# A decoder trunk on eight cores: the start of layer 0 reordered, the evictions of the convolution stage regrouped, and the norm at the head of the feed-forward part moved

## The chip, the cores and the metric

The kernel runs on the eight cores of one Trainium2 chip, which are two dies of four cores (0 to 3 and 4 to 7). Each core computes its own share of the requests, with the same program. The time is the device time of the slowest core in microseconds (us). A run is called slow where one die was over 1% longer than the other at a lower TensorE clock, or where it was over 1.5% above the fastest run of the same kernel.

The engines are named as in the profile: PE is TensorE, PEld its weight load, DVE is VectorE, ACT is ScalarE, POOL is GpSimd, and SP issues transfers (the page gives it no busy time, and the timeline shows its issues as SPq).

## The reference, cut to what matters

```python
def trunk(x, pool_prev, conv_prev, ffn_prev, pos0, p):
    for l in range(DEPTH):                                   # 4 layers
        h = rmsnorm(x, p['norm1'][l])
        z = h @ p['w_in'][l]                                 # 1024 -> 1792 columns, groups A, B, C
        a_out, pst = pool_mix(za, ...)                       # windows 2, 4, 8, 16
        b_out = spatial_gate(zu, zv, ...)                    # chunks of 128
        c_in = zc[..., :D_C] * jax.nn.sigmoid(zc[..., D_C:])
        c_conv, cst = causal_dwconv(c_in, conv_prev[l], ...) # depthwise, width 31
        c_out = jax.nn.silu(layernorm(c_conv, ...))
        x = x + jnp.concatenate([a_out, b_out, c_out], axis=-1) @ p['w_out'][l]
        h2 = rmsnorm(x, p['norm2'][l])
        up = h2 @ p['w_up'][l]                               # 1024 -> 2 x 2816
        gate_c, fst = causal_dwconv(gate, ffn_prev[l], ...)  # width 3
        x = x + (jax.nn.silu(gate_c) * val) @ p['w_down'][l]
    return rmsnorm(x, p['final_norm']), ...
```

A core holds 2048 prompt tokens and 64 sample tokens (x is kept transposed, 8 blocks of 128 channels). They are handled in five tiles: tiles 0 to 3 have 512 prompt tokens each, and tile 4 has the 64 sample tokens.

## The kernel before

A small scheduler in the program issues the instructions in order for each engine and works out the semaphore waits. A PSUM bank is marked as exclusive, so that a read of it also waits for every earlier read by another engine:

```python
    def _deps(self, reads, writes):
        for r in reads:
            if r.w is not None ...:      # wait for the last write
            if r.excl:                   # PSUM banks: wait for the other engines' reads too
                for s, v in r.r.items(): ...
```

**The start.** SP issues its loads in the order in which they are written here (from 1.06 us on; the state data at 22.97 and 25.40, the constants at 26.66). The tiny state data that the state casts need, and the constants of the pooling chains, are loaded behind most of x and of the staged weights:

```python
        load_x(4)
        S.dma("sp", VT[:, 0:VT_FW], vt_d[:, 0:VT_FW], DM["vt"], ...)     # norm gains
        for i in range(4):                                               # four f32 weights, cast later
            stage(X[:, :, 1024 + 256 * i : ...], [Res(f"stg{i}")])
            if i == 0:
                load_x(0, 0, 4); load_x(0, 4, 8)
        load_x(1, 0, 4); load_x(1, 4, 8)
        # ... (cut)
        stp = state_dma(0)                                               # sz, sc
        S.dma("sp", CST[:], cst_d, DM["cst"], ...)                       # constants
        nrm.first(4)                                                     # squares and sum of tile 4
        cast(0, "act", 0, 4); cast(0, "dve", 4, 8)                       # first weight to bf16
        nrm.apply(4, range(KC)); nrm.first(0); nrm.apply(0, range(KC))
        for i in range(1, 4): cast(i, "pool")
        # ... x tiles 2 and 3 behind the casts (cut)
        S.dma("pool", OBM[:], oneb_d, DM["obm"], ...)
        for t in range(6): bands.load(t)                                 # convolution matrices, 480 KB each
        # at the top of every layer:
            for j in range(3):                                           # state casts
                S.op("act", lambda e: e.copy(cin[j][:, 0:4, MB:MW], sc_v[...]), reads=[Rsc], writes=[Rcin[j]])
```

The projections of layer 0 then go by tile in the order 0, 4, 1, 2, 3, each tile through all five units (two for pooling, three for the gated convolution input), and each tile's norm just ahead of it. After the third convolution block's input has been sent through DRAM and back (a "hop", which transposes it), `prep_dma(0)` loads the spatial-gate matrices and `prep(0)` masks them on DVE.

**The convolution stage.** There are 12 steps. In each, PE forms two halves of 272 columns in two PSUM banks, and the result is needed as f32 (`y`), as bf16 (`yb`) and squared. The LayerNorm sums of a step (`stats`) are matmuls that run one step later:

```python
                for h in range(2):
                    cb = CVQ[:, 2 * q + h:2 * q + h + 1]
                    yh, ph, Rph = y[:, h * MW:(h + 1) * MW], pb2[h][0][:, 0:MW], pb2[h][1]
                    yb = ybf[:, 2 * (q % 2), h * MW:(h + 1) * MW]
                    if h == 0:
                        S.op("act", lambda e: e.activation(yh, ph, AF.Identity, bias=cb), ...)          # L795
                    else:
                        S.op("dve", lambda e: e.tensor_scalar(yh, ph, cb, None, ALU.add), ...)          # L797
                    S.op("dve", lambda e: e.tensor_scalar(yb, ph, cb, None, ALU.add), ...)              # L798
                b = 2 * (q % 2)
                S.op("act", lambda e: e.activation(ybf[:, b + 1, :], y, AF.Square), ...)                # L800
                if q >= 1:
                    stats(q - 1)                                                                        # PE, L755
```

**The head of the feed-forward part.** The last tile's norm is not finished when the up-projections begin. `tail2[0]` is its sum on PE (L415) with Ln and Exp on ACT, `tail2[1]` and `tail2[2]` scale its two halves on DVE. `up` leaves each unit's Silu pending until the next unit:

```python
                    for i, (f, ti) in enumerate(seq):
                        up(f, f, ti, w01[f], tail2[0] if i == 1 else None)    # between the two matmul groups of unit 1
                        if i == 2:
                            tail2[1]()
                        if i == 3:
                            tail2[2]()
```

Of the kernel before, what the change touches and what calls it, by code (L numbers as in the profile page):

```python
# [7 lines left out]
BF16 = mybir.dt.bfloat16  # L8
# [5 lines left out]
KC = 8  # L14
# [212 lines left out]
def build_nc():  # L227
# [39 lines left out]
    with ExitStack() as st:  # L267
# [57 lines left out]
        DXH = [S.dsem(f"dxh{t}") for t in range(2)]  # L325
# [45 lines left out]
        S.op("dve", lambda e: e.memset(EPST[:], EPS), writes=[Rones])  # L371
        load_x(4)
        S.dma("sp", VT[:, 0:VT_FW], vt_d[:, 0:VT_FW], DM["vt"], writes=[Rvt])
        for i in range(4):
            c = 1024 + 256 * i
            stage(X[:, :, c:c + 256], [Res(f"stg{i}")])
            if i == 0:
                load_x(0, 0, 4)
                load_x(0, 4, 8)
# [3 lines left out]
        class Norm:  # L383
            def __init__(self, base, gcol, final=False):
# [4 lines left out]
                sq_v, self.Rsq = AR.carve("sq", base + 256, 3 * 512, 3)  # L389
                self.sq = sq_v.rearrange("p (a n) -> p a n", a=3)  # L390
                self.ac, self.Rac = AR.carve("ac", base + 1792, 512, 1)
# [6 lines left out]
            def sqr(self, ti, m):  # L398
                c0, n = TTS[ti]
                q = self.q % 3  # L400
                self.q += 1
                sq = self.sq[:, q, 0:n]
                S.op("act", lambda e: e.activation(sq, X[:, m, c0:c0 + n], AF.Square), reads=[RX[m][ti]], writes=[self.Rsq[q]])  # L403
                if m == 0:
                    self.prev[ti] = (sq, self.Rsq[q])
                    return
                in0, R0 = self.prev[ti]
                dst, Rd = (self.ab[ti == 4][:, 0:n], self.Rab[ti == 4]) if m == KC - 1 else (self.ac[:, 0:n], self.Rac[0])
                S.op("pool", lambda e: e.tensor_tensor(dst, in0, sq, ALU.add), reads=[R0, self.Rsq[q]], writes=[Rd])  # L409
                self.prev[ti] = (dst, Rd)  # L410
# [14 lines left out]
            def apply(self, ti, kcs):  # L425
                c0, n = TTS[ti]
                ri, Rpb, i = self.ri[ti]
                for kc in kcs:
# [4 lines left out]
                    if self.final and kc % 4 == 3:  # L433
                        out_dma(y_o[:, kc - 3:kc + 1, c0:c0 + n], X[:, kc - 3:kc + 1, c0:c0 + n], [RX[k][ti] for k in range(kc - 3, kc + 1)], "y")
# [3 lines left out]
            def direct(self, ti, m):  # L438
                c0, n = TTS[ti]
                q = self.q % 3  # L440
                self.q += 1
                sq = self.sq[:, q].bitcast(BF16)[:, 0:n]
                S.op("act", lambda e: e.activation(sq, X[:, m, c0:c0 + n], AF.Square), reads=[RX[m][ti]], writes=[self.Rsq[q]])
# [10 lines left out]

            def first(self, ti, kcs=range(KC)):
                c0, n = TTS[ti]
                sqb = self.sq.rearrange("p a n -> p (a n)").bitcast(BF16).rearrange("p (a n) -> p a n", a=6)
                if kcs[0] == 0:
                    self.ri[ti] = bank(True)
                pb, Rpb, i = self.ri[ti]  # L460
                for kc in kcs:
                    q = kc % 3
                    eng = "act" if kc % 2 == 0 else "dve"
                    dst = sqb[:, 2 * q, 0:n]
                    src = X[:, kc, c0:c0 + n]
                    if eng == "act":
                        S.op("act", lambda e: e.activation(dst, src, AF.Square), reads=[RX[kc][ti]], writes=[self.Rsq[q]])
                    else:
                        S.op("dve", lambda e: e.tensor_tensor(dst, src, src, ALU.mult), reads=[RX[kc][ti]], writes=[self.Rsq[q]])
                    S.op("pe", lambda e: e.matmul(pb[:, 0:n], ONES[:], dst, start=(kc == 0), stop=(kc == KC - 1)),  # L470
                         reads=[self.Rsq[q], Rones], writes=[Rpb])
                if kcs[-1] == KC - 1:
                    self.rsq(ti, pb, Rpb, i)
# [48 lines left out]
        S.dma("sp", CST[:], cst_d, DM["cst"], writes=[Rcst])  # L522
        nrm.first(4)
        cast(0, "act", 0, 4)
        cast(0, "dve", 4, 8)
        nrm.apply(4, range(KC))
        nrm.first(0)
        nrm.apply(0, range(KC))
        for i in range(1, 4):
            cast(i, "pool")  # L530
        for t in (2, 3):
            after("sp", stages[2 * t - 4][1] + stages[2 * t - 3][1])
            load_x(t)
        S.dma("sp", VT[:, VT_FW:VT_N], vt_d[:, VT_FW:VT_N], DM["vt2"], writes=[Rvt2])
        const_dma(0)
        S.dma("pool", OBM[:], oneb_d, DM["obm"], writes=[Robm])
        qst = stq_dma(0)
        W.fill(5)
        bands = Bands(0)
        for t in range(6):  # L540
            bands.load(t)

        for l in range(DEPTH):
            sz_v, Rsz, sc_v, Rsc = stp
            QS, Rqs = qst
            cin, Rcin = [], []
            for j, a in enumerate((0, 4 * MW, 5308)):
                v, r = AR.carve(f"cin{j}", a, 4 * MW, 1)
                cin.append(v.bitcast(BF16).rearrange("p (f m) -> p f m", f=8))
                Rcin += r  # L550
# [6 lines left out]
            for j in range(3):  # L557
                S.op("act", lambda e: e.copy(cin[j][:, 0:4, MB:MW], sc_v[:, 64 * j:64 * j + 64].rearrange("p (f m) -> p f m", f=4)),
                     reads=[Rsc], writes=[Rcin[j]])
# [103 lines left out]
            def hop_in(j):  # L663
# [4 lines left out]
                S.dma("sp", hop1[j].rearrange("g (c f) m -> (g c) (f m)", f=8), cin[j].rearrange("p f m -> p (f m)"), DH1[j], reads=[Rcin[j]], writes=[Rh1[j]])  # L668
                S.dma("sp", Q[j][:, :, 4:4 + MW], hop1[j].rearrange("g p m -> p g m"), DQ[j], reads=[Rh1[j]], writes=[Rq[j][0]])

            if l == 0:
# [634 lines left out]
```

## Time and profile before

| | before |
|---|---|
| median of the first three runs | 2824.86 us (2819.37 to 3251.31) |
| profiled run, slowest core (4) | 2821.3 us |
| spans of die 0 / die 1 (medians) | 2791.5 / 2816.4 us |
| mean granted PE clock of die 0 / die 1 | 0.988 / 0.977 |
| PE busy | 2704.7 us, 96% |
| layer 0: first projection / first convolution matmul / start of the next stage | 23.6 / 138.6 / 172.2 us |
| convolution stage, layers 1 to 3 | 27.1, 27.5, 27.1 us |

The page, the table of stretches, the waits of PE and the timeline at the start are shown in the prediction below, where they are read. The stage starts in this table and further down are read from the trace as the start of the first matmul of each stage.

One part of the old profile is needed that the prediction only tells in words, the timeline of core 4 in the convolution stage of layer 1. Columns: start and length in us, engine and line, operation, out<-in, and in brackets the idle time before it and what ended it. First DVE, then ACT:

```profile
830.15 0.50 DVE L798 TENSOR_SCALAR arena<-ps,cvq_s 128x272 bf16<-128x272 f32 x1 [0.90 <-PE ps L755]
830.57 0.49 DVE L797 TENSOR_SCALAR arena<-ps,cvq_s 128x272 f32<-128x272 f32 x1
831.17 0.50 DVE L798 TENSOR_SCALAR arena<-ps,cvq_s 128x272 bf16<-128x272 f32 x1
832.50 0.50 DVE L798 TENSOR_SCALAR arena<-ps,cvq_s 128x272 bf16<-128x272 f32 x1 [0.83 <-PE ps L755]
...
831.15 0.66 ACT L800 ACTIVATE arena<-arena 128x544 bf16<-128x544 f32 x1 [1.11 <-DVE arena L797]
831.90 0.49 ACT L795 ACTIVATE arena<-ps,cvq_s 128x272 f32<-128x272 f32 x1
```

From one L798 to the same place a step later is 2.35 us, of which DVE works some 1.5. The bracket at 832.50 names PE's sums, but the program makes L798 wait until ACT's L795 has left the first half's bank: L795 ends at 832.39, and L798 begins 0.1 us later. L795 itself stands in ACT's queue behind the square L800 of the step before (831.15 + 0.66, L795 begins at 831.90), and L800 can't begin until DVE has written the second half (it stood 1.11 us). The sums on PE wait for both engines.

### The profile page before, as it was taken

To read this page: it belongs to the slowest core of one execution; us is meant where nothing else is said; L and a number is where in the kernel's file an instruction comes from. 1 tells how busy PE (TensorE), PEld (TensorE's weight loads), DVE (VectorE), ACT (ScalarE), POOL (GpSimd) and SP (SyncE) were. 2 spreads that over 40 slices of the span, in tenths; PEclk is the share of its full clock that TensorE was granted. 3 is DMA by queue.
4 is the path that set the end of the run, shared out by engine and by line. 5 is a ranking of instruction groups with operands and counts; after the bars stand their busy time and mean duration, and the time that the engine had idled before them with its cause. 6 is when DMAs were issued, how large, how long until landed. Compare 5 with 4: busy or idle time off the path is not lost.

```text
span 2821.3 us, 49230 instructions; the slowest of 8 cores (2789.2 to 2821.3 us)
## 1 busy us (share of the span) xinstructions
PE 2704.7 (96%) x15467; PEld 1317.9 (47%) x15735; DVE 1776.7 (63%) x3023; ACT 1436.0 (51%) x2758; POOL 535.5 (19%) x845
## 2 busy tenths in 40 slices
PE   4889999999999999999999999999999999999997
PEld 1354444444455444444445544444444644444443
DVE  3666755656685765656577576564668666555566
ACT  2354735447425572727634466372753647364573
POOL 1025100000603500000331430000041350000003
PEclk8899999999999999999999999999999999999998
DMA  9152412122445222221515322222242513122113
GB/s 227 63 113 39 68 30 44 29 46 44 80 90 112 34 37 36 42 38 31 93 38 105 83 48 35 45 35 38 38 79 65 121 30 58 32 45 41 31 36 124
DMA packets 82702, 170.97 MB, mean 61 GB/s; under 512 B 10960, under 2 KB 41936, under 8 KB 82384
## 3 DMA queue, kind: packets, MB, share of 16 engines
q0 software_dynamic: 31568, 108.44, 23.1%
q1 hardware_dynamic: 50880, 59.35, 7.0%
q8 instruction: 133, 2.18, 0.3%
q14 instruction: 121, 0.99, 0.1%
HBM read 250.37 MB, written 28.39 MB: 99 GB/s over the span
## 4 chain that ended last, share of the span: by engine, by line
PE 89%; DVE 4%; issue 3%; ACT 1%; DMA 1%; SPq 1%; POOL 0%; DVEq 0%; ACTq 0%; POOLq 0%
PE ps L1055 23%; PE ps L1049 22%; PE ps L981 15%; PE ps L1125 14%; PE ps L822 3%; PE ps L919 3%; PE ps L639 3%; PE ps L633 3%; PE ps L566 2%; DVE H L430 1%; SPq L138 1%; PE ps L905 1%; DVE arena L797 1%; DMA cstt<-cst 1%; PE ps L755 1%
## 5 line engine op out<-in xcount | busy, mean ns | idle before, releaser
L1055 PE MATMUL ps<-H,wsall 128*128 128x512 bf16 (+1 forms) x3500 | 707.9, 345 | 1.1
L1049 PE MATMUL ps<-H,wsall 128*128 128x512 bf16 (+1 forms) x3404 | 696.5, 344 | 6.2
L1069 DVE SCALAR_TENSOR_TENSOR arena<-arena,vt_s 128x512 f32<-128x512 f32 (+1 forms) x440 | 289.6, 658 | 406.4 <-ACT arena L1068 389.3
L1064 ACT COPY arena<-ps 128x512 f32<-128x512 f32 (+1 forms) x440 | 224.0, 509 | 582.8 <-PE ps L1049 534.3
L981 PE MATMUL ps<-arena,wsall 128*128 128x512 bf16 (+1 forms) x2515 | 474.7, 348 | 2.6
L1049 PEld LDWEIGHTS ps<-H,wsall 128*128 128x128 bf16 x3520 | 304.3, 99 | 339.7 <-issue 26.3
L1055 PEld LDWEIGHTS ps<-H,wsall 128*128 128x128 bf16 x3520 | 304.5, 99 | 339.0 <-issue 25.6
L1125 PE MATMUL ps<-arena,wsall 128*128 128x512 bf16 (+1 forms) x2200 | 399.0, 341 | 2.1
L1068 ACT ACTIVATE arena<-ps,vt_s 128x512 f32<-128x512 f32 (+1 forms) x440 | 309.2, 703 | 66.4 <-ACT arena L1064 3.0
L981 PEld LDWEIGHTS ps<-arena,wsall 128*128 128x128 bf16 x2560 | 217.9, 99 | 250.5 <-issue 44.4
L409 POOL TENSOR_TENSOR arena<-arena 128x512 f32<-128x512 f32 (+2 forms) x273 | 293.6, 1075 | 176.8 <-ACT arena L403 146.5
L1071 DVE SCALAR_TENSOR_TENSOR arena<-arena,vt_s 128x512 f32<-128x512 f32 (+1 forms) x440 | 289.6, 658 | 45.9 <-DVE arena L1069 0.2
L1128 DVE TENSOR_TENSOR X<-ps,X 128x512 f32<-128x512 f32 (+1 forms) x320 | 184.7, 596 | 196.9 <-PE ps L1125 196.9
L403 ACT ACTIVATE arena<-X 128x512 f32<-128x512 f32 (+1 forms) x312 | 168.0, 551 | 261.3 <-DVE X L983 146.9
L1125 PEld LDWEIGHTS ps<-arena,wsall 128*128 128x128 bf16 x2240 | 188.4, 98 | 211.5
L983 DVE TENSOR_TENSOR X<-ps,X 128x512 f32<-128x512 f32 (+1 forms) x320 | 185.0, 594 | 142.2 <-PE ps L981 132.4
L1082 DVE TENSOR_TENSOR arena<-arena 128x512 bf16<-128x512 bf16 (+1 forms) x440 | 261.3, 594 | 9.2 <-ACT arena L1064 4.1
L1081 ACT ACTIVATE arena<-arena 128x512 f32<-128x512 f32 (+1 forms) x440 | 246.0, 559 | 22.8 <-DVE arena L1071 22.7
L1074 ACT CAST arena<-ps 128x512 bf16<-128x512 f32 (+1 forms) x440 | 224.0, 509 | 65.3 <-PE ps L1055 57.1
L430 DVE SCALAR_TENSOR_TENSOR H<-X,vt_s,ps 128x512 bf16<-128x512 f32 (+1 forms) x320 | 208.3, 651 | 24.3 <-ACT ps L422 2.5
L1076 POOL COPY arena<-arena 128x2 f32<-128x2 f32 x88 | 17.4, 198 | 1007.9 <-ACT arena L1064 1007.9
L138 POOL DMA_DIRECT2D wsall<-wup x88 | 46.6, 533 | 441.6 <-PE ps L1125 276.4
(105 smaller groups left out, 2026.3 us busy)
## 6 DMA issues: line engine op xcount, KB each, us to landing
wsall<-wup POOLq DMA_DIRECT2D x88, 512.0 KB, 5.7
arena<-bnd POOLq DMA_DIRECT2D x32, 480.0 KB, 16.8
wsall<-wdn POOLq DMA_DIRECT2D x32, 448.0 KB, 5.0
hop<-arena SPq DMA_DIRECT2D x24, 544.0 KB, 3.4
arena<-hop SPq DMA_DIRECT2D x24, 544.0 KB, 4.1
wsall<-wout POOLq DMA_DIRECT2D x16, 512.0 KB, 12.5
wsall<-wdn POOLq DMA_DIRECT2D x16, 512.0 KB, 5.1
y_o<-X SPq DMA_DIRECT2D x8, 1024.0 KB, 4.2
```

What stands on the lines that cost most here:

```text
L409: S.op("pool", lambda e: e.tensor_tensor(dst, in0, sq, ALU.add), reads=[R0, self.Rsq[q]], writes=[Rd])
L430: S.op("dve", lambda e: e.scalar_tensor_tensor(dst[:, kc, c0:c0 + n], X[:, kc, c0:c0 + n], VT[:, self.gcol + kc:self.gcol + kc + 1], ri, A ...
L981: S.op("pe", lambda e: e.matmul(pb[:, 0:n], lh, rh, start=(q == 0), stop=(q == len(ops) - 1)), reads=rr, writes=[Rpb], inc=(q == len(ops) ...
L1049: S.op("pe", lambda e: e.matmul(pg[:, 0:n], wv[:, k, 0:128], H[:, k, c0:c0 + n], start=(k == 0), stop=(k == 7)), reads=[Rw, RH[k][ti]], wr ...
L1055: S.op("pe", lambda e: e.matmul(pv[:, 0:n], wv[:, k, 128:256], H[:, k, c0:c0 + n], start=(k == 0), stop=(k == 7)), reads=[Rw, RH[k][ti]], ...
L1064: S.op("act", lambda e: e.copy(G[:, gc:gc + n], pg[:, 0:n]), reads=[Rpg], writes=[gw_])
L1068: S.op("act", lambda e: e.activation(T_, pg[:, 0:n], AF.Identity, bias=fb, scale=w2), reads=[Rpg, Rvt2], writes=[Rtm[q]])
L1069: S.op("dve", lambda e: e.scalar_tensor_tensor(T_, G[:, gc - sh:gc - sh + n], w1, T_, ALU.mult, ALU.add), reads=gr_ + [Rvt2], writes=[Rtm[q]])
L1071: S.op("dve", lambda e: e.scalar_tensor_tensor(T_, G[:, gc - 2 * sh:gc - 2 * sh + n], w0, T_, ALU.mult, ALU.add), reads=gr_ + [Rvt2], writ ...
L1081: S.op("act", lambda e: e.activation(T_, T_, AF.Silu), reads=[Rtm[q]], writes=[Rtm[q]])
L1082: S.op("dve", lambda e: e.tensor_tensor(actb[:, fl, c0:c0 + n], VB_, T_, ALU.mult), reads=[Rvst[q], Rtm[q]], writes=[Rab[fl * 5 + ti]])
L1125: S.op("pe", lambda e: e.matmul(pb[:, 0:n], w[1][:, kk, m2 * 128:(m2 + 1) * 128], actb[:, kk, c0:c0 + n], start=(kk == 0), stop=(kk == nf ...
```

## The change

The intent is to take away standing time of PE without changing the arithmetic that it does: (a) layer 0 loads and projects in the order in which data can arrive, (b) the masks are prepared inside the stage, (c) each PSUM bank of the convolution stage is read by one engine only and the buffers are tracked by halves, (d) the norm sum in the feed-forward part moves one unit later, with the first Silu held back, (e) the sum at the layer head moves between two matmul groups and the last store is cut in two. The core of the diff, with cuts marked:

```diff
+        load_x(0, 0, 4)
+        load_x(0, 4, 8)
+        S.dma("sp", VT[:, 0:VT_FW], vt_d[:, 0:VT_FW], DM["vt"], writes=[Rvt])
+        stage(X[:, :, 1024:1280], [Res("stg0")])
         load_x(4)
-        S.dma("sp", VT[:, 0:VT_FW], vt_d[:, 0:VT_FW], DM["vt"], writes=[Rvt])
-        ... (weights 0 to 3, x tile 0 behind the first)
+        S.dma("sp", CST[:], cst_d, DM["cst"], writes=[Rcst])
+        stage(X[:, :, 1280:1536], [Res("stg1")])
         load_x(1, 0, 4)
         load_x(1, 4, 8)
 ... (cut: eight bf16 buffers for squares, squares on DVE as well as ACT)
+        def late_loads():
+            after("pool", [RX[k][3] for k in (0, 7)])          # bands wait for the last x tile
+            ... (OBM, small states, bands, prep_dma(0), further weights)
 ...
-                S.op("act", lambda e: e.copy(cin[j][:, 0:4, MB:MW], sc_v[...]), reads=[Rsc], writes=[Rcin[j]])
+                S.op("pool", lambda e: e.tensor_copy(cin[j][:, 0:4, MB:MW], sc_v[...]), reads=[Rsc], writes=[Rcs[j]])
 ...
             if l == 0:
-                for pos, ti in enumerate(order0):              # tile by tile, all units
-                    ... (cut)
-                prep_dma(0)
-                prep(0)
+                run(("a", 0, 0), ("a", 1, 0), ("c", 0, 0), ("c", 0, 4), ("sq", 1, al), ("mm",), ("n", 1, al), ("c", 1, 0), ...
+                    ... (cut: by arrival of tiles and weights; "P" is a pooling chain, "h" a hop)
+                    ("a", 0, 3), ("a", 1, 3), "P", ("c", 1, 3), ("h", 1), "P", ("c", 2, 3), ("h", 2))
 ...
-                for h in range(2):
-                    ... (the loop shown above)
+                S.op("act", lambda e: e.activation(y[:, sl[0]], ph[0], AF.Identity, bias=cbs[0]), ...)              # L786
+                S.op("act", lambda e: e.activation(ybf[:, b + 1, sl[0]], ph[0], AF.Square, bias=cbs[0]), ...)       # L787
+                S.op("dve", lambda e: e.tensor_copy(ybf[:, b, sl[0]], y[:, sl[0]]), reads=Ry0, ...)                 # L788
+                S.op("dve", lambda e: e.tensor_scalar(y[:, sl[1]], ph[1], cbs[1], None, ALU.add), ...)              # L789
+                S.op("act", lambda e: e.activation(ybf[:, b + 1, sl[1]], y[:, sl[1]], AF.Square), reads=Ry1, ...)   # L790
+                S.op("dve", lambda e: e.tensor_scalar(ybf[:, b, sl[1]], ph[1], cbs[1], None, ALU.add), ...)         # L791
 ...
+                if q == 6 and l == 0:
+                    prep(0)
 ...
-            def up(f, fl, ti, w, mid=None):
+            def up(f, fl, ti, w, mid=None, hold=False):
 ...
-                flush()
-                fst["pend"] = stage2
+                if not hold:
+                    flush()
+                fst["pend"].append(stage2)
 ...
-                        up(f, f, ti, w01[f], tail2[0] if i == 1 else None)
+                        up(f, f, ti, w01[f], tail2[0] if i == 2 else None, i == 1)
```

## The prediction

In (c), the terms for the copy and for the square of 272 columns are cut from the sum of one step, which came to 1.73 us; the stage was forecast from PE's 1.80 us, which is larger. An estimate from the trace of before gives the same 1.73: ACT's L403 took 0.63 us for 512 columns and 0.25 for 64, so a square of 272 instead of 544 takes about 0.66 - 0.23 = 0.43; DVE took 0.69 us for a cast of 1024 columns and 0.17 for a copy of 32 (L1063), so a copy of 272 takes about 0.30; neighbours overlap by 0.08 us on DVE (L798 and L797 at 830.15) and by 0.09 on ACT (L422 and L1064 at 955.20, core 0).

That matmuls are slower after a gap rests on the two rates read at 52.55 and 82.70; how long this lasts, and what lowers the clock of a die, was not shown. Groups of eight at 2.10 us stand where the granted clock was 0.81 (459.3 to 464.0 us on core 4, with 1.00 on both sides). A table load on ACT, which (d) speaks of, takes 1.28 us in this trace (L421, 11 times). The 4 us of ramp in (a) is the author's estimate; the two small first transfers of before, 40 and 256 KB, took 4.0 and 4.6 us from issue to landing.

> **What bounds the kernel now.** I read the page first: its engine table says which engine is full, and its slices say where it isn't.
>
> ```profile
> PE 2704.7 (96%) x15467; PEld 1317.9 (47%) x15735; DVE 1776.7 (63%) x3023; ACT 1436.0 (51%) x2758; POOL 535.5 (19%) x845
> ...
> PE   4889999999999999999999999999999999999997
> ```
>
> TensorE is the bound of the program as a whole. The change removes almost no matrix work, so it can win only where TensorE stands still: 2821.3 - 2704.7 = 117 us at most, plus matmuls that ran at a low clock. The low digits are in the first three slices and the last. Next, the busy time by stretch (columns: stretch; its length; busy us of PE, PEld, DVE, ACT, POOL; PE clock; DMA share; GB/s):
>
> ```profile
> 0.00:138.50 138.50, 84.98 (x354) 34.24 (x361) 71.08 (x117) 44.81 (x83) 10.93 (x18) 0.84 0.57 146
> 138.50:172.20 33.70, 24.51 (x263) 19.27 (x261) 19.18 (x39) 12.63 (x23) 9.96 (x33) 0.88 0.80 143
> ...
> 1497.00:1531.00 34.00, 29.12 (x291) 21.13 (x290) 23.17 (x46) 14.29 (x26) 9.32 (x32) 1.00 0.63 123
> ```
>
> The first row is layer 0 up to its convolution stage (53.5 us idle), the second that stage (9.2 us idle), the third about the same stage of layer 2 (4.9 us idle). Then the waits of PE over the whole span:
>
> ```profile
> PE ps L470 <- ACT arena L467: 26.8, 5, 11.5
> PE ps L755 <- DVE arena L798: 22.2, 39, 7.0
> PE ps L415 <- DVE arena L1063: 9.2, 4, 2.3
> PE ps L566 <- DVE H L430: 8.6, 13, 2.4
> PE ps L639 <- DVE H L430: 6.2, 1, 6.2
> ```
>
> L470 is the first norm, waiting for squares; L755 the LayerNorm sums of the convolution stage; L415 the norm sum at the head of each feed-forward part, 2.3 us in each of four layers. Last, the timeline near the start (start and length in us; in brackets the idle time before and what ended it):
>
> ```profile
> 43.63 0.54 ACT L558 CAST arena<-arena 128x64 bf16<-128x64 f32 x3 [21.00 <-DMA arena<-stc]
> ...
> 47.55 1.14 ACT L467 ACTIVATE arena<-X 128x512 bf16<-128x512 f32 x2
> ...
> 48.32 0.59 PE L470 MATMUL ps<-arena,ones 128*128 128x512 bf16 x1 [11.49 <-ACT arena L467]
> ...
> 52.55 3.62 PE L633 MATMUL ps<-H,wsall 128*128 128x512 bf16 x8
> ...
> 82.70 1.89 PE L639 MATMUL ps<-H,wsall 128*128 128x512 bf16 x8
> ```
>
> ACT works in order, stood 21 us before three tiny state casts whose data was late in the load queue, and so held the squares that PE needed. The last two lines show the same work at two rates.
>
> [...] about 428 ns from start to start at 52.55 after a gap, 216 ns at 82.70. [...] this trace has groups of eight at 2.10 us instead of 1.73 (ratio 0.82)[...]. [...] the cast of 128x1024 here took 694 ns[...].
>
> **The change part by part.**
>
> *(a) Loads and order of layer 0.* Tile 0 now loads before everything, the constants and the small state before the later weights, the state casts go to POOL, the bulky band matrices wait until all of X is in, and projections are ordered by arrival. Before, X by itself moved at about 3.6 us per MB (the halves of tile 0 arrive at 14.7 and 18.3), the staged weights at 3.9 (casts start at 21.15, 25.28, 29.00). Summing the new queue at these rates, after some 4 us of ramp: tile 0 is in at 11.5 us; first weight 15.5, tile 4 at 17, second weight 21, tile 1 at 28, third weight 33, fourth 37, tile 2 at 44, tile 3 at 51. A POOL cast adds 1.9 us to each weight. Squares and Ln/Exp of tile 0 take 3.3 us; scaling takes 8 x 0.84 = 6.7 us on DVE, so it ends at 21.7. Real projections start near 19 (23.6 before). PE still waits for tile 1 and the third weight (about 29 to 35.5). After that I walk the queues in program order. DVE is the tighter one: from 21.7 on it has tile 4's scaling (3.0), three scalings of 6.7 (20.1), twelve gate products of 1.1 (13.2), four pairs of pooling chains of 2.4 + 4.0 (25.6, and 1.0 more for tile 0), tile 4's small work (5.6): 68.5 us. With about 11 us of gaps (gates of tile 0, norm 1, norm 2) it ends at 101. PE's own need is 256 matmuls x 0.216 = 55 for the projections, 7 for norm sums and 2 for tile 4, 64 us, which fits inside. So the gate of the third channel block ends at 101 (before: convolution matmuls began at 138.6).
>
> *(b) prep(0).* Before, its loads were issued only at 140.45, landed at 145.9, and DVE, in order, kept the first convolution results waiting: 7.0 us. Now the loads are early and the two operations (0.69 + 0.42) come in the middle of the stage. Minus 7.0, plus at most 1.1.
>
> *(c) Convolution loop, all four layers.* Two engines read one PSUM bank before, and the schedule makes such reads wait for one another. Before, per step: ACT Identity 0.48, then DVE 0.50, DVE 0.49, then ACT Square of 544 elements 0.66, and around again: 2.13 us, and the steps in the trace are 2.14 to 2.35. After: Identity 0.48, semaphore about 0.1, copy of 272 elements from SBUF [...], add 0.49, 0.1, Square of 272 [...]: 1.73 us. PE needs 2 x 0.66 + 0.48 = 1.80 us per step, so PE becomes the bound, at about 1.87. In layers 1 to 3, from the first matmul of the stage to the first of the next is 27.2 us now (823.2 to 850.4); 12 x 1.87 + 0.8 = 23.2. Minus 4 each, 12 us for three; the PE waits there (4.2, 4.8, 4.0) say the same.
> Layer 0: from 101, with the first three steps already computed but not evicted, 11 x 1.87 + 0.8 gives the next stage's start at 122.5; before it was 172.2. That is 49.7; I take off 4.7 for waits that my walk doesn't see: **minus 45 for layer 0**, (b) and its (c) included.
>
> *(d) Feed-forward head.* The norm sum moves one tile later, behind 16 more matmuls (3.46 us), against a wait of 2.3: the wait goes, minus 9.2 in four layers. Holding the first Silu back keeps Ln/Exp ahead of the table switch; three temporaries suffice.
>
> *(e) Small ones.* The norm sum at the layer head moves behind eight 64-column matmuls (0.25 us) in three layers: minus 0.7. The last store is halved to 512 KB: at 3.6 us per MB, minus 1.8. Finer buffers for squares and y remove waits already counted.
>
> Sum: 45 + 12 + 9.2 + 0.7 + 1.8 = 68.7. 2824.9 - 68.7 = **2756 us**, 2.4% less.
>
> **The rivals.** (1) The start stays bound: DVE collects more gaps than I see, [...] and the hop through DRAM (3.4 + 4.1 us plus issue) delays the convolution. For it: DVE is about 85% full in my walk, so each late operand shifts all. Against: DVE was only 71 of 138.5 us busy before. Layer 0 would give 25 instead of 45: 2776. (2) The loop in (c) doesn't speed up, because six small operations carry more semaphore latency than four large ones: 2756 + 16 = 2772. For it: the 1.73 and 1.80 are close. Against: DVE no longer waits for ACT to leave a PSUM bank. (3) The clock gives back: die 1 has a mean clock of 0.977 against 0.988 and is 25 us longer; as much again on the slow die would make 2770 to 2780. (4) PE, not DVE, paces layer 0, and the stage starts 8 us earlier: 2748.
>
> **Range and chances.** Layer 0 carries two thirds of the sum with perhaps 12 us either way, the clock another 10. Eight in ten: 2735 to 2782. The 2% line is at 2768.4, 12 us above my number: faster 0.76, within 2% 0.23, slower 0.01.
>
> **What would show it.** (a) holds if the first convolution matmul stands near 97 to 104 us, DVE is over 75% busy between 20 and 100 us, and waits of PE on squares are under 10 us; fails if it starts after 115. (b): no 7 us wait before the first L755 sum. (c): steps of about 1.9 us and under 2 us of such waits per layer; fails if they remain at 2.1. (d): no 2.3 us wait of the norm sum. (e): the last store shorter. The total would be wrong if the mean clock of the slow die falls below 0.97, or if new waits appear in the feed-forward head.

## The result, and the profile after

The changed kernel ran 14 times on that chip. Six runs were fast, from 2744.17 to 2759.36 us, with a mean of 2750.8 (12 fast runs of before: 2822.0). The median of all 14: 2843.89 us; before had 15 runs in all with a median of 2822.42 us. The ratio is 0.975 with a 95% interval of 0.9734 to 0.9766. Here and below, a ratio is the mean time of one kernel's fast runs over the mean of the other kernel's fast runs of the same rounds, so it isn't quite the ratio of the medians.

The page of the profiled run, whose slowest core was again core 4 (2746.7 us), answers to the first fence of the prediction:

```profile
PE 2682.5 (98%) x15467; PEld 1312.5 (48%) x15735; DVE 1762.3 (64%) x3014; ACT 1438.6 (52%) x2801; POOL 541.1 (20%) x858
...
PE   6899999999999999999999999999999999999997
```

Standing time of PE fell from 2821.3 - 2704.7 = 116.6 us to 2746.7 - 2682.5 = 64.2 us, which is 52 us. The other 22 us of the 74.6 are busy time: PE does the same 15467 matmuls, at a higher clock on average (0.986 against 0.975 on core 4). The table of stretches (columns: stretch, its length, busy us of PE, PEld, DVE, ACT, POOL, then PE clock, DMA share, GB/s):

```profile
0.00:102.90 102.90, 78.08 (x355) 32.15 (x362) 66.16 (x107) 45.21 (x87) 15.03 (x25) 0.96 0.78 195
102.90:127.60 24.70, 21.75 (x260) 17.82 (x260) 17.92 (x41) 15.12 (x35) 7.27 (x26) 1.00 0.72 159
1449.00:1474.00 25.00, 20.94 (x249) 17.11 (x247) 15.80 (x38) 15.76 (x36) 8.52 (x29) 1.00 0.71 129
```

These are the same three places as before: layer 0 up to its convolution stage, that stage, and the one of layer 2. The first row shrank from 138.5 us to 102.9, and its PE clock rose from 0.84 to 0.96, with less standing of PE between the matmuls (24.8 us against 53.5). The waits of PE over the whole span:

```profile
PE ps L456 <- ACT arena L448: 17.8, 5, 11.9
PE ps L768 <- DMA arena<-hop: 4.6, 4, 1.7
PE ps L745 <- DVE arena L791: 3.1, 5, 0.8
PE ps L745 <- DVE arena L788: 1.6, 1, 1.6
PE ps L815 <- DMA wsall<-win: 1.5, 1, 1.5
```

Line numbers moved: L456 is the norm sum that was L470, L745 are the LayerNorm sums that were L755, and L431 is the scaling that was L430. The sums of the convolution stage went from 22.2 us to 4.7, and the 9.2 us of L415 are gone. Of the 17.8 us of the norm sum, 11.9 are the very first wait, until x has come in. A new entry is the wait for the hop through DRAM (L768).

The timeline of the convolution loop after the change, in layer 3, answers to the one of before:

```profile
2128.12 0.30 DVE L788 CAST arena<-arena 128x272 bf16<-128x272 f32 x1 [0.46 <-PE ps L745]
2128.34 0.49 DVE L789 TENSOR_SCALAR arena<-ps,cvq_s 128x272 f32<-128x272 f32 x1
2129.95 0.30 DVE L788 CAST arena<-arena 128x272 bf16<-128x272 f32 x1 [0.51 <-PE ps L745]
2131.73 0.30 DVE L788 CAST arena<-arena 128x272 bf16<-128x272 f32 x1 [0.46 <-PE ps L745]
...
2129.30 0.49 ACT L786 ACTIVATE arena<-ps,cvq_s 128x272 f32<-128x272 f32 x1
...
105.14 1.06 DVE L642 TENSOR_TENSOR arena<-ps,arena 128x512 bf16<-128x512 f32 x1
106.69 0.30 DVE L788 CAST arena<-arena 128x272 bf16<-128x272 f32 x1 [0.19 <-ACT arena L787]
```

A step takes 1.83 and 1.78 us, and the copy takes 0.30 us. The brackets name PE's sums again, but L788 copies what ACT's L786 has written: L786 ends at 2129.79, and L788 begins 0.16 us later. So DVE still waits for ACT once in each step, for some 0.5 us, but for a result and no longer for a bank that ACT has to leave. The last two lines are from layer 0: DVE finishes its last gate product (L642) at 106.2 and takes up the convolution loop only at 106.69, almost 4 us after PE began the convolution at 102.90.

The stages on the slowest core, read from the trace's first matmul of each stage. A feed-forward part is counted from its first up-projection to the start of its last down-projection, a layer head from the first projection to the first convolution matmul, and the last row from the start of the last matmul:

| core 4, us | before | after | difference | predicted |
|---|---|---|---|---|
| first projection begins | 23.6 | 19.8 | | 19 |
| first convolution matmul of layer 0 | 138.6 | 102.9 | | 97 to 104 |
| end of the convolution stage of layer 0 | 172.2 | 127.6 | -44.5 | -45 |
| convolution stages of layers 1 to 3 | 27.1, 27.5, 27.1 | 23.4, 25.9, 22.4 | -10.0 | -12 |
| feed-forward parts, four layers (sum) | 1686.7 | 1668.8 | -17.8 | -9.2 |
| layer heads of layers 1 to 3 | 176.6 | 175.5 | -1.1 | -0.7 |
| after the last matmul | 12.9 | 11.5 | -1.4 | -1.8 |
| sum | | | -74.8 | -68.7 |

On core 0, whose die has the higher clock, the feed-forward parts went from 416.8, 418.5, 418.5, 418.5 to 415.2 in all four layers, which is 11.6 us. The rest of the 17.8 on core 4 comes with the mean clock of its die, which rose from 0.977 to 0.987.

The head of the feed-forward part on core 0, before, shows where the 11.6 come from:

```profile
953.97 0.38 PE L415 MATMUL ps<-arena,ones 128*128 128x512 bf16 x1 [2.29 <-DVE arena L1063]
954.18 3.35 PE L1055 MATMUL ps<-H,wsall 128*128 128x512 bf16 x8
959.32 1.89 PE L1055 MATMUL ps<-H,wsall 128*128 128x512 bf16 x8
...
952.45 1.26 POOL L409 TENSOR_TENSOR arena<-arena 128x512 bf16<-128x512 f32 x1 [0.89 <-ACT arena L1064]
```

The wait is 2.29 us, and the eight matmuls after it take 3.35 us where eight usually take 1.89: PE ran below its full rate for a moment after the pause (the granted clock is 1.00 in the pause and 0.57 from 954.0 to 957.4 us). On this core the three feed-forward parts with such slow matmuls took 418.5 us and the one without 416.8, so they cost 1.7 us. They don't always follow: of the 32 such waits in this trace (eight cores, four layers, each 2.29 to 2.31 us), 21 were followed by eight slow matmuls, three of four on core 0 and one of four on core 5. The wait is put down to DVE's L1063, but the last operand of the sum is POOL's addition of squares L409, which ends at 953.71, just before PE goes on; the name in brackets is that of an event near it, not of the cause. The same head on core 0 after the change:

```profile
921.80 1.89 PE L1042 MATMUL ps<-H,wsall 128*128 128x512 bf16 x8
...
924.37 1.89 PE L1048 MATMUL ps<-H,wsall 128*128 128x512 bf16 x8 [0.67 <-DVE arena L1056]
...
920.92 3.30 DVE L431 SCALAR_TENSOR_TENSOR H<-X,vt_s,ps 128x512 bf16<-128x512 f32 x4
924.13 0.17 DVE L1056 COPY arena<-fb 128x32 f32<-128x32 f32 x1
```

No half rate any more, but a new wait of 0.67 us. It ends when DVE's second half of the scaling does, at 924.2: the scaling reads the norm's factor from a PSUM bank, and the program gives that bank back to PE with the last scaling.

### The profile page after: what moved, and what is told of

It is laid out like the page before. It is cut to its first block, busy times and chain, and to the rows that moved or that the text cites. A ratio compares the mean times of both kernels' runs of the same rounds, so it can differ in the third digit from the quotient of the medians.

```text
span 2746.7 us, 49364 instructions; the slowest of 8 cores (2719.5 to 2746.7 us)
## 1 busy us (share of the span) xinstructions
PE 2682.5 (98%) x15467; PEld 1312.5 (48%) x15735; DVE 1762.3 (64%) x3014; ACT 1438.6 (52%) x2801; POOL 541.1 (20%) x858
## 3 DMA queue, kind: packets, MB, share of 16 engines
q0 software_dynamic: 31568, 108.44, 23.7%
## 4 chain that ended last, share of the span: by engine, by line
PE 91%; DVE 4%; DMA 2%; issue 2%; ACT 1%; POOL 0%; DVEq 0%; SPq 0%; ACTq 0%; POOLq 0%
PE ps L1048 23%; PE ps L1042 23%; PE ps L974 16%; PE ps L1118 14%; PE ps L815 3%; PE ps L912 3%; PE ps L628 2%; PE ps L634 2%; DVE H L431 1%; PE ps L561 1%; DMA arena<-hop 1%; PE ps L898 1%; DVE arena L598 1%; PE ps L768 1%; DVE arena L642 1%
## 5 line engine op out<-in xcount | busy, mean ns | idle before, releaser
L1048 PEld LDWEIGHTS ps<-H,wsall 128*128 128x128 bf16 x3520 | 303.5, 98 | 336.4 <-issue 17.8
L974 PEld LDWEIGHTS ps<-arena,wsall 128*128 128x128 bf16 x2560 | 218.1, 99 | 250.5 <-issue 44.3
L1064 DVE SCALAR_TENSOR_TENSOR arena<-arena,vt_s 128x512 f32<-128x512 f32 (+1 forms) x440 | 289.5, 658 | 47.3 <-DVE arena L1062 1.8
L1074 ACT ACTIVATE arena<-arena 128x512 f32<-128x512 f32 (+1 forms) x440 | 245.5, 559 | 26.5 <-DVE arena L1064 25.9
L431 DVE SCALAR_TENSOR_TENSOR H<-X,vt_s,ps 128x512 bf16<-128x512 f32 (+1 forms) x320 | 208.3, 651 | 34.3 <-ACT ps L423 12.5
```

The costliest lines, as they stand in the source:

```text
L431: S.op("dve", lambda e: e.scalar_tensor_tensor(dst[:, kc, c0:c0 + n], X[:, kc, c0:c0 + n], VT[:, self.gcol + kc:self.gcol + kc + 1], ri, A ...
L974: S.op("pe", lambda e: e.matmul(pb[:, 0:n], lh, rh, start=(q == 0), stop=(q == len(ops) - 1)), reads=rr, writes=[Rpb], inc=(q == len(ops) ...
L1048: S.op("pe", lambda e: e.matmul(pv[:, 0:n], wv[:, k, 128:256], H[:, k, c0:c0 + n], start=(k == 0), stop=(k == 7)), reads=[Rw, RH[k][ti]], ...
L1064: S.op("dve", lambda e: e.scalar_tensor_tensor(T_, G[:, gc - 2 * sh:gc - 2 * sh + n], w0, T_, ALU.mult, ALU.add), reads=gr_ + [Rvt2], writ ...
L1074: S.op("act", lambda e: e.activation(T_, T_, AF.Silu), reads=[Rtm[q]], writes=[Rtm[q]])
```

## The experiments

All kernels gave correct results. They ran on chips whose two dies were alike: the fast runs of before have means of 2797.0, 2794.4 and 2795.1 us. Ratios are to before, by fast runs. Stage lengths are the medians of the eight cores of the profiled run. "Before" in stage lengths is the profile of the first chip (medians of the eight cores: first convolution matmul 136.6 us, end of that stage 170.8, convolution stages 34.1, 27.4, 27.5 and 27.1), and for the feed-forward parts its die 0, since these differ with the clock (1672.3 us in four layers on core 0 at 0.989, 1686.7 on core 4 at 0.975).

### The parts alone

**Loop only.** The kernel before with the new evictions of the convolution stage:

```diff
-                    S.op("dve", ... tensor_scalar(yb, ph, cb, ...)) for both halves, Square of 544 columns
+                    ... the six operations L786 to L791, buffers tracked by halves
```

> The kernel before with the new convolution loop alone. Theory (two engines taking turns on one PSUM bank and on one y buffer set the step): steps of the sums fall from 2.14-2.35 us to about 1.87, the stage of layers 1 to 3 from 27.2-27.6 us to 22.5-24 each; layer 0 keeps its 7 us wait for the mask loads. Whole time 4 x 3.5 = 14 us less, ratio 0.995. Rival 1 (the gain in that stage comes from the other parts of the change): the stage stays above 26 us, ratio 0.999 or more. Rival 2 (the time moves into the wait for the hop through DRAM): the sums stop waiting but the stage stays above 25.5 us and PE waits at the convolution matmuls for the hop.

It took 2782.2 us in the mean of its fast runs, ratio 0.9947 (0.993 to 0.9963), which is 14.8 us less than before. The stages are 30.7, 23.7, 24.9 and 23.7 us. That agrees with the theory of one engine for each bank, but this run changes the banks, the split of the square and the buffers together; the shared-bank run below changes the bank alone. Two lines of the waits of PE (core 5) show what remained in the stages:

```profile
PE ps L755 <- DVE arena L798: 7.4, 1, 7.4
...
PE ps L778 <- DMA arena<-hop: 6.4, 3, 3.0
```

The first is the mask preparation of layer 0, which this kernel leaves where it was (part (b) of the prediction, 7.0 us there). The second is why layer 2 stays above the expected 24 us, and it is new: once the loop is faster, PE reaches the third block before its hop has come back.

**Feed-forward head only.**

```diff
-                        up(f, f, ti, w01[f], tail2[0] if i == 1 else None)
+                        up(f, f, ti, w01[f], tail2[0] if i == 2 else None, i == 1)      # and the list of pending Silus
```

> The kernel before with the feed-forward head alone changed (norm sum one tile later, first Silu held). Theory: the 2.3 us wait of the norm sum vanishes in all four layers; in layers 1 to 3 the half-rate matmuls that followed it vanish too, so from the first up-projection to the last down-projection 1.6 us less in layer 0 and 3.3 us less in layers 1 to 3 on an undisturbed die: 11.6 us in all, ratio 0.996. Rival (only the wait itself, as predicted): 2.3 less in each, 9.2 in all, ratio 0.9967. Rival 2: the wait comes back elsewhere in the head, ratio 0.999.

2783.8 us, ratio 0.9952 (0.9934 to 0.9969). The interval is too wide to tell 9.2 from 11.6 us, but the stages tell it: all four feed-forward parts take 415.2 us, against 416.8 in layer 0 and 418.5 in the others before on an undisturbed die. That is 1.6 + 3 x 3.2 = 11.3 us. Layer 0 gains only the wait (2.3 - 0.7), the others the half rate too.

**Start only.** The changed kernel with loop, head, layer head and store undone:

```diff
-  (changed kernel) L786 to L791, hold of the first Silu, sum of the layer head between two groups, halved store
+  (kernel before)  L795 to L800, no hold, sum ahead of them, one store
```

> The kernel after with the new convolution loop, feed-forward head, layer head and last store undone: the new start of layer 0 with the early masks alone. Theory (the parts add): the first convolution matmul stays at 98 to 104 us, layer 0's next stage starts at 131 to 134 us instead of 172.2, all later stages are as before; 38 to 42 us less, ratio 0.9855. Rival (the finer loop is needed for the start's gain to reach the end, as the transfers and DVE would otherwise meet the old loop): less than 32 us, ratio 0.989 or more.

2753.3 us, ratio 0.9843 (0.9829 to 0.9858), which is 43.7 us. The first convolution matmul stands at 99.2 us and the stage ends at 128.7, earlier than expected. The changed kernel's own stage, run again on the later chip, ends at 126.5. So in layer 0 the faster loop is worth some 2 us only. DVE still has gate products until about 106 us there, as the two lines of layer 0 above show, and until then its share of the evictions can't begin.

### Taking the start apart

The named wait at the start, ACT's 21.00 us ahead of the state casts, asks to be removed first.

**State casts on POOL**, the one line of the change that the profile points to:

```diff
-                S.op("act", lambda e: e.copy(cin[j][:, 0:4, MB:MW], sc_v[...]), reads=[Rsc], writes=[Rcin[j]])
+                S.op("pool", lambda e: e.tensor_copy(cin[j][:, 0:4, MB:MW], sc_v[...]), reads=[Rsc], writes=[Rcs[j]])
```

> The kernel before with nothing but the three state casts moved from ACT to POOL. Theory (ACT, in order, was held until 43.6 us by late data, and with it the squares of tile 1): the 11.5 us wait of PE before 48 us shrinks to 3 us or less, tile 1 scales earlier, and since tiles 2 and 3 arrive only at about 70 us and DVE waits for the constants too, just 3 to 8 us of it reach the first convolution matmul; ratio 0.997 to 0.999. Rival 1 (this wait was the whole of the start's loss): 20 us or more less, ratio 0.993 or lower. Rival 2 (the constants of pooling, loaded behind, hold DVE at the same place anyway): nothing, ratio 1.000.

2795.0 us, ratio 0.9993 (0.9979 to 1.0006): nothing, and the first convolution matmul stands at 136.4 us where it was at 136.6. My theory missed, and the rival, that the constants hold DVE just as long, held. From the timeline of DVE on core 5:

```profile
50.98 0.75 DVE L607 SCALAR_TENSOR_TENSOR arena<-arena,cstt 128x512 f32<-128x512 f32 x1 [17.43 <-DMA cstt<-cst]
```

and from the waits of PE of the same kernel:

```profile
PE ps L470 <- DVE arena L469: 17.8, 3, 15.8
```

DVE stands 17.43 us in its first pooling chain, until the constants have landed, and the squares that DVE makes for the norm sum are queued behind it. In the kernel before, this wait was hidden: on core 4 DVE stood 15.61 us for a copy in ACT's queue, which was behind the late state casts, and then only 1.59 us more for the constants. The profile named the wait that ended last.

**Constants early as well.**

```diff
         S.dma("sp", VT[:, 0:VT_FW], vt_d[:, 0:VT_FW], DM["vt"], writes=[Rvt])
+        S.dma("sp", CST[:], cst_d, DM["cst"], writes=[Rcst])
 ...
         stp = state_dma(0)
-        S.dma("sp", CST[:], cst_d, DM["cst"], writes=[Rcst])
```

> The kernel before with the state casts on POOL and, besides, the constants loaded right behind the first small vector. Theory (the start of the kernel before is a row of waits, each hidden by the one ahead of it: state casts, then constants, then x tiles 2 and 3): the 15.8 us wait of PE for DVE squares goes, tile 1 is scaled by about 55 us instead of 70 to 74, but the squares of tile 2 still wait for x at about 70 us; the first convolution matmul comes at 128 to 134 us (136.5 before), ratio 0.997 to 0.999. Rival 1 (the constants were the last wait that counts): at 118 us or earlier, ratio 0.994 or lower. Rival 2 (the order of the projections alone holds it): 136 us, ratio 1.000.

Half of its six runs were slow. The three fast ones have a mean of 2792.6 us, ratio 0.999 (0.997 to 1.001). The first convolution matmul stands at 134.5 us, 2 us earlier, just beyond the weak end of what I expected. Again another wait took the place, in the timeline of ACT on core 7:

```profile
70.06 1.67 ACT L444 ACTIVATE arena<-X 128x512 bf16<-128x512 f32 x3 [15.95 <-DMA X<-xt]
```

Now the squares of x tile 2 wait 15.95 us for the tile itself.

**Band matrices behind x as well**, since they are loaded at the same time:

```diff
+        after("pool", [RX[k][3] for k in (0, 7)])
         S.dma("pool", OBM[:], oneb_d, DM["obm"], writes=[Robm])
```

> As the run before it, and the band matrices and the other loads on POOL wait until the last x tile is in. Theory (x tiles 2 and 3 share the DMA engines with the bands in the kernel before and come at 70 us and later for this): they land by 43 to 52 us, and the first convolution matmul comes at 105 to 116 us, with the old order of projections; ratio 0.988 to 0.992. Rival 1 (as the kernel after showed no effect of the bands, they have none here): as without it, 128 to 134 us, ratio 0.997 to 0.999. Rival 2 (the order of projections gives nothing): it reaches the 100 us of the kernel after, ratio 0.986.

2783.1 us, ratio 0.9957 (0.9933 to 0.9981). The first convolution matmul stands at 124.9 us and the stage ends at 159.0. I had expected 105 to 116, so this missed too: the bands are worth 10 us here, not 20 to 30. Of ACT's waits for x before 136 us (core 2) the longest is now 5.3 us, where one was 15.95. The row is thus 136.6, 136.4, 134.5, 124.9, and about 100 with the whole new start. The last 25 us belong to what is left of part (a): tile 0 first, projections by arrival, and each norm ahead of need. I haven't divided these further.

**Bands early in the changed kernel**, the same wait taken away on the other side:

```diff
         def late_loads():
-            after("pool", [RX[k][3] for k in (0, 7)])
             S.dma("pool", OBM[:], oneb_d, DM["obm"], writes=[Robm])
```

> The kernel after, with the band matrices and other late loads issued as soon as POOL is through its casts (about 40 us) and not after the last x tile (52 us). Theory (DVE is full from 40 us on and sets the pace of layer 0, and x tiles 2 and 3 arrive with little to spare): the tiles land later by about 4 and 10 us, the first convolution matmul comes 0 to 4 us later than in the kernel after (about 100 us), ratio 0.975 to 0.977. Rival (keeping transfers apart is what made the start faster): 10 us or more later, ratio 0.979 or more. Rival 2: earlier, since the hop and bands then don't meet: ratio 0.974.

2728.6 us, ratio 0.9764 (0.975 to 0.9778), with the first convolution matmul at 99.9 us, as in the changed kernel (99.4 on such a chip). In the new order the early bands cost nothing that these runs can see, and in the old order they cost 10 us. In the profile of the changed kernel, no engine of any core waits for x between 30 and 110 us but POOL, which holds the bands back for it (11.3 to 13.9 us), so the tiles land before anything else needs them. With the early bands, PE's waits on ACT's squares stay as they were (18.2 us on core 3, 17.8 in the changed kernel), while in the kernel with the constants early ACT stood the 15.95 us shown above for x tile 2.

### One bank, two engines

**Shared bank.** The changed kernel, with DVE taking the bf16 first half from PSUM again:

```diff
-                S.op("dve", lambda e: e.tensor_copy(ybf[:, b, sl[0]], y[:, sl[0]]), reads=Ry0, writes=[Ryb[2 * b]])
+                S.op("dve", lambda e: e.tensor_scalar(ybf[:, b, sl[0]], ph[0], cbs[0], None, ALU.add), reads=[R0, Rcvq], writes=[Ryb[2 * b]])
```

> The kernel after, but the bf16 copy of the first half is made by DVE from the PSUM bank again (0.50 us) instead of from y in SBUF (0.30 us); everything else, the finer buffers too, stays. Theory (two engines reading one bank take turns, and that sets the step): DVE can start only when both ACT reads of the bank are done, the step goes from 1.79 us back to 2.2 or 2.3, the stage of layers 1 to 3 from about 23 to 27 or 28 us, 15 to 20 us in all, ratio 0.981. Rival (only the number and size of operations counts: DVE has 1.5 us of work in a step of 1.8): the step stays below 1.9, ratio 0.975 to 0.976.

2753.9 us, ratio 0.9855 (0.9835 to 0.9875), which is (0.9855 - 0.9759) x 2795 = 27 us more than the changed kernel takes. The stages take 31.9, 30.3, 30.4 and 30.1 us, longer than those of layers 1 to 3 before. The timeline of DVE on core 0:

```profile
790.42 0.50 DVE L788 TENSOR_SCALAR arena<-ps,cvq_s 128x272 bf16<-128x272 f32 x1 [0.98 <-ACT arena L787]
...
792.91 0.50 DVE L788 TENSOR_SCALAR arena<-ps,cvq_s 128x272 bf16<-128x272 f32 x1 [0.97 <-ACT arena L787]
```

One operand changed, and the step went from about 1.8 to 2.49 us. DVE must let ACT leave the bank, and ACT now reads it twice (L786, L787), so DVE stands 0.97 us at each step. The mechanism is as the theory says, and stronger than the 2.2 to 2.3 us that I expected. The run shows that a shared bank alone costs more than the whole gain of the new loop; it doesn't divide that gain between the bank, the split square and the finer buffers.

### The head of the feed-forward part

**No hold.** The changed kernel with the norm sum one unit later, but the first Silu not held back:

```diff
-                        up(f, f, ti, w01[f], tail2[0] if i == 2 else None, i == 1)
+                        up(f, f, ti, w01[f], tail2[0] if i == 2 else None)
```

> The kernel after without holding the first Silu back in the feed-forward head. Theory (two more table loads of 1.28 us on ACT while it has to empty PSUM): the first up to the last down projection becomes 0.5 to 2 us longer in each layer than the 415.2 us of the kernel after, ratio 0.9755 to 0.978. Rival (ACT has slack there, the hold is idle): 415.2 us as before, ratio 0.975.

2740.0 us, ratio 0.9805 (0.9791 to 0.9819). The feed-forward parts take 418.9, 417.3, 418.8 and 417.3 us, so the whole gain of this part is lost. From the timeline of ACT on core 0:

```profile
911.15 1.28 ACT L1074 ACT_TABLE_LOAD   x1
912.45 0.26 ACT L1074 ACTIVATE arena<-arena 128x64 f32<-128x64 f32 x1
912.72 1.28 ACT L422 ACT_TABLE_LOAD   x1
914.02 0.66 ACT L422 ACTIVATE ps<-ps,epst 128x512 f32<-128x512 f32 x1
917.22 1.28 ACT L1074 ACT_TABLE_LOAD   x1
```

A single small Silu (L1074) ahead of Ln and Exp (L422, and L423 right behind it) makes ACT load three tables where the changed kernel loads one in the same place (at 912.72 us, behind Ln and Exp). Each load takes 1.28 us, and the next operation starts 1.29 or 1.30 us after the load does. The scaling begins later by that, and so does the return of the norm's bank. From the waits of PE:

```profile
PE ps L1048 <- DVE arena L1056: 10.6, 4, 2.8
```

It is the wait of 0.67 us seen above, grown to 2.8 in the worst of the four.

**Spread head.** The scaling of the last tile cut into four pieces, over four units, to remove that wait:

```diff
-                        if i == 2:
-                            tail2[1]()
-                        if i == 3:
-                            tail2[2]()
+                        if 2 <= i < 6:
+                            tail2[i + 1]()          # two of the eight blocks each
```

> The kernel after with the scaling of the last tile in the feed-forward head spread over four units of work (two pieces each) instead of two (four each). Theory (the wait removed from the norm sum is given back in part: 3.3 us of scaling in one piece holds DVE, thus Silu, thus the emptying of PSUM, and PE waits 0.67 us in each layer): that wait goes, 414.5 us instead of 415.2 in each layer, 2.7 us in all, ratio 0.974. Rival (the wait is for something else, such as a bank still held by a norm): 415.2 us stays, ratio 0.975.

The feed-forward parts take 414.75 us instead of 415.17 and the wait is gone from the list. That is 1.7 us in four layers, too little for the times: 2726.6 us, ratio 0.9757 (0.9743 to 0.9771).

### A version meant to be better, and the changed kernel again

**Combined.** The spread head, the third hop sent to DRAM ahead of the last pooling chains of layer 0, and the last two band loads two steps later:

```diff
-                    ("a", 0, 3), ("a", 1, 3), "P", ("c", 1, 3), ("h", 1), "P", ("c", 2, 3), ("h", 2))
+                    "P", ("c", 1, 3), ("h", 1), ("c", 2, 3), ("o", 2), ("a", 0, 3), ("a", 1, 3), "P", "P", ("h", 2))
 ...
-                if q in (1, 2):
-                    bands.load(5 + q)
+                if q in (3, 4):
+                    bands.load(3 + q)
```

> The kernel after with three additions: in layer 0 the last channel block goes out to DRAM before the last pooling chains, not behind them; in all layers the last two band loads are issued two steps later, out of the way of the last hop; and the scaling in the feed-forward head is spread over four units. Theory (the hop is the new wait of the convolution stage, and meets these band loads): waits of PE for the hop and for the last input weights fall below 1 us a layer, the stage takes 23.5 to 25.5 us in layer 0 (27 to 28 in the kernel after) and 22.4 to 23 in the others (23 to 24.9), the head 414.75 us; 5 to 8 us less than the kernel after, ratio to the kernel before 0.9735. Rival (a later band load comes too late and its matmuls wait): the stage becomes longer by 1 to 3 us in each layer, ratio 0.977.

**The changed kernel once more**:

> The kernel after, unchanged, on the same chip and in the same rounds as the three above, so that the last version can be compared with it. Ratio to the kernel before 0.975 to 0.9765, first convolution matmul at 99 to 102 us, its stage 27 to 28 us in layer 0 and 23 to 25 in the others, 415.2 us in the feed-forward part.

The combined version took 2726.4 us, ratio 0.9753 (0.9736 to 0.977). The changed kernel took 2727.9 us, ratio 0.9759 (0.9742 to 0.9776). The intervals overlap almost wholly, so no gain is shown. The stage of layer 0 took 27.3 us in both. On core 0 of the combined version another wait stands where that for the hop had been (L751 are the LayerNorm sums, L794 is the copy):

```profile
PE ps L751 <- DVE arena L794: 3.3, 1, 3.3
```

The hop had not been the only limit of layer 0: DVE's backlog, which ends at 106.99 us here, took its place, and the stage stayed as long. The later band loads didn't shorten the stage of layers 1 to 3 (23.5, 24.2 and 22.3 us against 22.8, 23.4 and 23.0).

## Why the prediction was right

The prediction was 2756 us, and the fast runs have a mean of 2750.8, inside its range and 5 us below its number. About 3 of the 5 us lie in the base: 2824.9 was the median of three runs of which one was slow, and the fast runs of before have a mean of 2822.0. For a comparison without the difference of the dies I take the kernel with the state casts on POOL in place of before (its ratio to before is 0.9993) against the changed kernel run again, both on chips with equal dies, as medians of the eight cores:

| us | casts on POOL | changed again | difference | predicted |
|---|---|---|---|---|
| end of the convolution stage of layer 0 | 170.8 | 126.5 | -44.3 | -45 |
| convolution stages of layers 1 to 3 | 81.7 | 69.1 | -12.6 | -12 |
| feed-forward parts, four layers | 1671.4 | 1660.7 | -10.7 | -9.2 |
| layer heads of layers 1 to 3 | 175.4 | 174.1 | -1.3 | -0.7 |
| after the last matmul | 13.0 | 11.5 | -1.5 | -1.8 |
| sum | | | -70.4 | -68.7 |

The differences are of medians by layer and add up to a little too much: the median spans of these two runs differ by 68.3 us, and the means of their fast runs by 67.1.

Point by point:

- **(a), the start.** Its sum was right, and its details were partly off. DVE is the tighter engine, as said: it was busy 58.76 of the 80 us from 20 to 100 (73%, against "over 75%"), and 56.73 of 66.70 us (85%) from 40 to 106.7. Its end came at 106.2 us rather than 101. The scaling of tile 0 ended at 24.5 instead of 21.7, and two idle stretches of 4.67 and 5.95 us stand before 40 us, about the 11 that the walk allowed; the remaining 2 to 3 us I haven't traced. The 4.7 us taken off "for waits that my walk doesn't see" just covered it; that the size fitted is luck, since no wait had been named for it. The sign "waits of PE on squares under 10 us" was put badly: they are 17.8 us, of which 11.9 is the first load.
- **(a), which part of it.** The prediction told the 21 us of ACT as if their removal would release PE. The casts alone gave nothing (ratio 0.9993). The gain came only from several waits removed together, each of which had hidden behind the next: casts, constants, x behind the bands, order.
- **(b)** held. The wait of 7 us is absent in the changed kernel, and stands at 7.4 us in the loop-only kernel.
- **(c)** held. The step came out at 1.78 to 1.83 us against 1.87 and the copy at 0.30 us; the shared-bank experiment shows that turns on one bank are by themselves enough to make the stage slower than before. In layer 2 on core 4 the gain was only 1.7 us, since PE had to wait for the hop and for a weight there. Rival (2), more semaphore latency, is false.
- **(d)** is the term that was mis-sized in both directions. The wait of 2.3 us went in four layers, but 0.67 of it came back as a wait for the norm's bank, and the half rate that followed the wait in three of four layers, 1.7 us each (418.5 against 416.8), was left out of the sum, although the prediction reads both rates, 428 and 216 ns, from the trace. On core 0 that makes 4 x 1.63 + 3 x 1.7 = 11.6 against 9.2; elsewhere it depends on how many waits the half rate followed. The head-only and no-hold runs show that the hold belongs to it: without it nothing is gained.
- **(e)** held within 0.6 us for each item (1.3 and 1.5 us against 0.7 and 1.8), but no run tests it alone.
- **Rival (3), the clock gives back,** is false in the fast runs: the mean clock of die 1 rose from 0.977 to 0.987 (0.981 to 0.997 on the cores of all six fast runs), at 98% PE in the profiled one. Rival (1) overrated the gaps, and rival (4), PE pacing layer 0, would have had the convolution begin 8 us earlier, which it didn't.

What stays open: how the last 25 us of the start divide between tile 0 first and the new order; and the wait for the hop in layer 2, which varies between cores and runs (that stage took 22.5 to 26.8 us on single cores of the changed kernel's two profiles). Why eight of the 14 first runs of the changed kernel were slow, against three of the 15 of before, isn't settled either; on the later chip four of five of its runs were fast.

## What to carry to other kernels

In a kernel whose TensorE is full, add up where it stands still, by stage, and expect little else but what a steadier clock gives back (here 22 of 74.6 us). Waits of different engines hide one another, so the one that the profile names may be worth nothing by itself (here ACT's 21 us, ratio 0.9993): follow the queue behind it and remove the row together. Let one engine read each PSUM bank where the result is needed in several forms, and take the other form from the SBUF copy (here 1.8 us a step against 2.49); and when a wait is moved behind other work, move with it what it would collide with, here the Silu that would bring two more table loads of 1.28 us.
